# Gate stage of a residual block in one fixed order on four engines, with 23 instead of 19 chunks of the first expert product ahead

## The chip, the core and the metric

The kernel runs on one core of a Trainium2 chip. The metric is the device time of one execution in microseconds (us); three runs of the kernel before gave 1525.38, 1526.84 and 1527.6, their median is 1526.84.

## What is computed

Input is one sequence of 512 tokens of width 1024, in fp32. The block adds to it a mixture of spatial gating and banded attention, and then a PEER layer, which is where the change lies:

```python
def block(xb):                                   # for each of four blocks of 128 tokens
    q = (xb @ w_query).reshape(128, 8, 2, 128)
    sc = einsum('thpd,hpkd->thpk', q, sub_keys)
    s_top, i_top = top_k(sc, 16)
    cand = s_top[:, :, 0, :, None] + s_top[:, :, 1, None, :]        # 256 sums per head
    best, pos = top_k(cand, 16)
    eidx = ...                                   # i_top of one half * 128 + i_top of the other, at pos
    g = softmax(best)
    h = gelu(einsum('thkd,td->thk', expert_u[eidx], xb))
    return einsum('thk,thkd->td', g * h, expert_v[eidx])
```

There are 8 heads, 128 keys in each half of a head and so 16384 experts; a token uses 16 of them per head.

## The kernel before

**The work.** Tokens lie in four tiles of 128. For tiles 1 to 3 (384 tokens) the PEER layer is dense: the hidden value of all 16384 experts is computed, multiplied by a gate that is zero for experts not chosen, and multiplied by all rows of `expert_v`. For tile 0 the chosen rows are gathered from memory instead (`gather_u`, `gather_v`, lines 777 to 792, tile `row`, a ring of ROW buffers; POOL issues a gather, DVE reads the row). Of tile 3 the last 64 tokens get their hidden values by gathers too, early, in the gate stage (`gather_early` and `dots_early`, lines 472 and 481, tile `rowe`, a ring of four buffers): 64 gathers in all. The first product therefore covers 320 tokens.

**The products.** Every fp32 product is three products of a rounded part hi and a rest lo. `load_split` (lines 110 to 118) brings a weight tile of 512 KB by SP's DMA queue into `raw`, ACT writes hi (line 116) and DVE or POOL writes lo (line 117, "the split"). There are three raw and five hi and lo buffers. The first product has 64 chunks of two tiles of 128 experts. A tile is 24 matmuls of 128x320 (lines 132 to 134) and a gelu on ACT (line 518), which leaves it in an `act` buffer. The second product (lines 811 to 847) takes a chunk of act, multiplies it by the gates `gc` (line 825), makes hi and lo of it (`wh` line 826, `wl` lines 827 and 832), and adds 36 matmuls of 128x512 into six accumulators (`pa`, `px`).

**The stages.** First the mixture (not touched). Then the routing: for each head `candidates` makes the scores and the best 16 keys of both halves and, in between, one chunk of the first product; `choose` finds the best 16 of the sums, one head later. Behind the last choice (head 7) comes the gate stage: 48 steps of 8 tokens. A step makes two one-hots from the chosen experts' numbers, `bm` for the lower 7 bits (DVE line 689, then multiplied by the gate on POOL, line 690) and `am` for the upper (DVE line 697; on odd steps below SOON = 28 it is ACT, lines 694 and 695), multiplies them on PE (line 704), copies the result to `gst` (ACT, line 707), and every fourth step 2 MB of gst go to memory (`gd`, line 710, ACT's queue). With the steps go early gathers and their reads, and tiles of the first product: nine chunks come with the routing and its start, and ten more, up to AHEAD = 19, here. `gates_of` (line 661) turns a token tile's experts and gates by transposes (line 671) ahead of its 16 steps. Last comes the stage of the second products: each chunk's second product, then the first product of the chunk AHEAD later, and beside them the routing of tile 0 (`route_gathered`, in two parts) and its 256 gathers. A second product needs `gc`, which SP's queue reads back from gd (768 KB for two chunks, line 814).

**What sets the order.** PE runs in the order in which the program is written, in the gate stage and behind it. On DVE, ACT, POOL and SP a scheduler places instructions by its own estimate of when they are ready; each engine and each DMA queue then runs its own list in that order. In the gate stage, PE's list has BRIDGE = 4 tiles of the first product ahead of the first transposes, then ten over steps 0 to 27; the last six (LAST = 3 chunks) are written behind the steps and the scheduler puts them among the later ones:

```python
want = (len(early) + max(0, SOON - n) - 1) // max(1, SOON - n)    # early gathers of step n
gather_early(want)
...
while filled < min(last, begun + (last - begun) * (n + 1) // SOON):   # tiles up to step n
    next(fill)
    filled += 1
```

Of the kernel before, what the change touches and what calls it, by code (L numbers as in the profile page):

```python
# [26 lines left out]
NH = 8  # L27
# [30 lines left out]
ROW = 6  # L58
ROWE = 4
LAGE = 2  # L60
BRIDGE = 4
EARLY = 3
LEAD = 2
SOON = 28
AHEAD = 19
LAST = 3
FILL = 1
# [3 lines left out]
ROUTE = 8  # L71
GB = 4
TC = 8
TG = 32
# [8 lines left out]
def hybrid_block(tc, x, ln1, w_in, gng, wsT, bsb, qkg, bias, w_out, ln2, wq, skT, uT, ud, vd, out):  # L83
    nc = tc.nc
    ctx = ExitStack()
    with ctx:
# [408 lines left out]
        def weights_early():  # L495

            own = slice(P - UX, P)
            d = du.rearrange("p (a k) -> p a k", k=TOPK)
            nc.vector.tensor_copy(dots[own, :, 0, :], d[own])
            nc.scalar.dma_start(dots[own, :, 1, :], d[0:P - UX])  # L500
            nc.scalar.activation(dots[own], dots[own], AF.Gelu_apprx_tanh)
            nc.vector.tensor_tensor(gate[own, TT - 1, :], gate[own, TT - 1, :],
                                    dots[own].rearrange("p a b k -> p (a b k)"), op=ALU.mult)

        def first_product(c):
            for _ in first_products(c, nc.vector):
                pass

        def first_products(c, eng, whole=False):
            act = actp.tile([P, BC, NDU], F32, name="act", tag="act", bufs=AHEAD + 1)  # L510
            acts[c] = act
            for b in range(BC):
                hi, lo = load_split(uT[c * BC + b], eng, b=P)
                ps = pu()
                for k in range(KT):
                    x2 = (xbh[:, k, T0:T0 + NDU], xbl[:, k, T0:T0 + NDU]) if whole else (xch[:, k, :], xcl[:, k, :])
                    mm3(ps[:, :NDU], (hi[:, k, :], lo[:, k, :]), x2, k == 0, k == KT - 1)
                nc.scalar.activation(act[:, b, :], ps[:, :NDU], AF.Gelu_apprx_tanh)  # L518
                yield
# [25 lines left out]
        def pairs(pool, top, pos, n):  # L545
# [12 lines left out]
            tree = pool.tile([P, n, TOPK, 32], F32, name="tree", tag="tree", bufs=1)  # L558
            nc.gpsimd.tensor_copy(tree, cand[:, 1, :, None, 0:32].to_broadcast([P, n, TOPK, 32]))
            return cand, tree  # L560

        def choose(pool, cand, tree, n, best, to, mask):

# [32 lines left out]
        def candidates(h):  # L596
# [14 lines left out]
            fill = itertools.chain(*[first_products(len(acts) + i, nc.gpsimd, True) for i in range(FILL)])  # L611
# [18 lines left out]
        for _ in first_products(0, nc.vector, True):  # L630
            pass
        cands = []
        for h in range(NH + 1):
# [4 lines left out]
            if h < NH:  # L638
                cands.append(candidates(h))
            if h > 0:  # L640
# [107 lines left out]
        for _ in fill:  # L748
            pass
# [167 lines left out]
```

## Time and profile before

| | |
|---|---|
| median of three runs | 1526.84 us |
| the profiled execution: its own time | 1521.59 us |
| the profiled execution: its span, first to last instruction | 1519.8 us |
| PE busy | 1401.5 us (92%) |
| DVE busy | 1174.2 us (77%) |
| ACT busy | 628.8 us (41%) |
| POOL busy | 659.5 us (43%) |
| moved by DMA | 396.77 MB, mean 261 GB/s |
| mean granted clock of PE | 0.972 of 2.4 GHz |

The profile is that of one execution. Its span is what all times in the rows are measured in; 1.8 us of the execution's own time lie outside it. The shares are averages over stages with different limits, so rows of single stretches tell more than these do: the routing ends near 454 us, the gate stage near 645, and from 661 to the end only second and first products and the gathers of tile 0 run.

### The profile page before, as it was taken

What the parts mean: (1) busy time and instruction counts of PE and PEld (TensorE: products, weight loads), DVE (VectorE), ACT (ScalarE), POOL (GpSimd) and SP (SyncE); (2) the same over time, 40 slices, a digit from 0 to 9 for tenths busy, and PEclk for the clock granted to TensorE, in tenths of its full rate; (3) what the DMA queues carried; (4) which work ended last, traced back from release to release, by engine and by line L of the source; (5) the groups of instructions that cost most, each with busy time, mean ns of one, the idle gap of its engine ahead of it and who ended that gap; (6) DMA issues with size and microseconds to landing.
All of it is one profiled execution on the core that took longest, in us unless ns stands there. A gap on an engine that the chain in (4) does not pass through costs nothing.

```text
span 1519.8 us, 21632 instructions
## 1 busy us (share of the span) xinstructions
PE 1401.5 (92%) x7801; PEld 1236.7 (81%) x7801; DVE 1174.2 (77%) x2342; ACT 628.8 (41%) x1052; POOL 659.5 (43%) x434
## 2 busy tenths in 40 slices
PE   7999999989738679869999999999999999999988
PEld 6886678978728679859888898989898989888876
DVE  5437454879999888759998888888887888867774
ACT  5457544332237665424343334333333333333331
POOL 0000025566538755504645654665445554524420
PEclk9999999999978899979999999999999999999999
DMA  5352234467558968767989999899999999977972
GB/s 181 110 180 70 94 132 150 125 200 236 172 192 273 339 211 249 208 207 266 375 284 367 347 366 375 328 357 367 349 337 352 341 350 331 349 261 295 343 271 103
DMA packets 163419, 396.77 MB, mean 261 GB/s; under 512 B 12080, under 2 KB 74544, under 8 KB 163312
## 3 DMA queue, kind: packets, MB, share of 16 engines
q1 hardware_dynamic: 65968, 200.30, 37.5%
q0 software_dynamic: 46432, 168.60, 29.9%
q10 hardware_dynamic: 50912, 26.49, 6.2%
q8 instruction: 61, 1.00, 0.2%
q14 instruction: 46, 0.38, 0.1%
HBM read 363.86 MB, written 31.46 MB: 260 GB/s over the span
## 4 chain that ended last, share of the span: by engine, by line
PE 63%; DVE 17%; DMA 9%; issue 6%; ACT 3%; POOL 2%; DVEq 0%; SPq 0%; POOLq 0%
PE pu L132 8%; PE pu L134 8%; PE pu L133 8%; PE pa L842 6%; PE pa L843 6%; PE pa L846 6%; DMA rowe<-in_ud,eui 3%; DMA gc<-gd 3%; PE px L846 3%; PE px L842 3%; PE px L843 3%; PE pa L704 2%; PE pa L132 2%; PE pa L134 2%; PE pa L133 2%
## 5 line engine op out<-in xcount | busy, mean ns | idle before, releaser
L116 ACT ACTIVATE hi<-raw 128x1024 fp32r<-128x1024 f32 x300 | 317.8, 1060 | 596.0 <-DMA raw<-in_vd 179.4
L117 DVE TENSOR_TENSOR lo<-raw,hi 128x1024 fp32r<-128x1024 f32 x268 | 332.6, 1242 | 100.0 <-ACT hi L116 97.5
L790 POOL DMA_INDIRECT row<-in_vd,eint x128 | 212.9, 1663 | 195.8 <-DVE acc L792 167.8
L132 PE MATMUL pu<-xch,hi 128*128 128x320 f32 x880 | 273.6, 311 | 4.3 <-ACT act L518 4.2
L134 PE MATMUL pu<-xch,lo 128*128 128x320 f32 x880 | 271.9, 309 | 3.0 <-DVE lo L117 2.8
L133 PE MATMUL pu<-xcl,hi 128*128 128x320 f32 x880 | 271.8, 309 | 0.0
L779 POOL DMA_INDIRECT row<-in_ud,eint x128 | 181.3, 1417 | 180.4 <-DVE row L781 145.7
L842 PE MATMUL pa<-hi,wh 128*128 128x512 f32 x512 | 201.1, 393 | 0.0
L843 PE MATMUL pa<-lo,wh 128*128 128x512 f32 x512 | 200.6, 392 | 0.0
L132 PEld LDWEIGHTS pu<-xch,hi 128*128 128x128 f32 x880 | 166.0, 189 | 7.5 <-ACT act L518 5.6
L134 PEld LDWEIGHTS pu<-xch,lo 128*128 128x128 f32 x880 | 165.9, 189 | 4.0 <-DVE lo L117 4.0
L133 PEld LDWEIGHTS pu<-xcl,hi 128*128 128x128 f32 x880 | 166.1, 189 | 1.6
L792 DVE SCALAR_TENSOR_TENSOR acc<-row,hw,acc 128x1024 f32<-128x1024 f32 x128 | 164.2, 1283 | 0.2
L846 PE MATMUL pa<-hi,wl 128*128 128x512 f32 x512 | 158.8, 391 | 0.4 <-DVE wl L832 0.4
L781 DVE SCALAR_TENSOR_TENSOR row<-row,xb 128x1024 f32<-128x1024 f32 x128 | 155.7, 1219 | 2.4 <-DMA row<-in_ud,eint 2.4
L704 PE MATMUL pa<-bm,am 128*128 128x128 f32 x768 | 101.0, 292 | 36.3 <-DVE bm L689 12.2
L704 PEld LDWEIGHTS pa<-bm,am 128*128 128x128 f32 x768 | 96.4, 205 | 40.5 <-issue 14.1
L825 DVE TENSOR_TENSOR act<-act,gc 128x320 f32<-128x320 f32 x128 | 54.8, 486 | 88.2 <-DMA gc<-gd 88.2
L842 PE MATMUL px<-hi,wh 128*128 128x512 f32 x256 | 100.9, 394 | 15.9 <-ACT wh L826 15.9
L846 PEld LDWEIGHTS pa<-hi,wl 128*128 128x128 f32 x512 | 96.5, 189 | 21.6 <-DVE wl L832 1.1
L842 PEld LDWEIGHTS pa<-hi,wh 128*128 128x128 f32 x512 | 96.9, 189 | 20.6
L843 PEld LDWEIGHTS pa<-lo,wh 128*128 128x128 f32 x512 | 96.9, 189 | 20.6
(211 smaller groups left out, 2521.6 us busy)
## 6 DMA issues: line engine op xcount, KB each, us to landing
raw<-in_uT SPq DMA_DIRECT2D x128, 512.0 KB
raw<-in_vd SPq DMA_DIRECT2D x128, 512.0 KB
gd<-gst ACTq DMA_DIRECT2D x12, 2048.0 KB
gc<-gd SPq DMA_DIRECT2D x32, 768.0 KB
raw<-in_w_in SPq DMA_DIRECT2D x20, 512.0 KB
raw<-in_wq SPq DMA_DIRECT2D x16, 512.0 KB
raw<-in_w_out SPq DMA_DIRECT2D x8, 512.0 KB
bt<-in_bias SPq DMA_DIRECT2D x8, 256.0 KB
```

The costliest lines, as they stand in the source:

```text
L116: nc.scalar.activation(hi, raw, AF.Copy)
L117: eng.tensor_tensor(lo, raw, hi.bitcast(F32), op=ALU.subtract)
L132: nc.tensor.matmul(ps, lh[0], rh[0], start=first, stop=False)
L133: nc.tensor.matmul(ps, lh[0], rh[1], start=False, stop=False)
L134: nc.tensor.matmul(ps, lh[1], rh[0], start=False, stop=last)
L704: nc.tensor.matmul(ps[:, i * P:(i + 1) * P], am[:, 4 * q + i, :], bm[:, 4 * q + i, :], start=True, stop=True)
L779: nc.gpsimd.indirect_dma_start(out=row, out_offset=None, in_=ud, in_offset=bass.IndirectOffsetOnAxis(ap=eint[:, j:j + 1], axis=0))
L790: nc.gpsimd.indirect_dma_start(out=row, out_offset=None, in_=vd, in_offset=bass.IndirectOffsetOnAxis(ap=eint[:, j:j + 1], axis=0))
L792: nc.vector.scalar_tensor_tensor(acc0, row, hw[:, j:j + 1], acc0, op0=ALU.mult, op1=ALU.add)
L842: nc.tensor.matmul(accs[t][half], wh[:, b, tok], w[b][0][:, ds_], start=first, stop=False)
L843: nc.tensor.matmul(accs[t][half], wh[:, b, tok], w[b][1][:, ds_], start=False, stop=False)
L846: nc.tensor.matmul(accs[t][half], wl[:, b, tok], w[b][0][:, ds_], start=False, stop=last)
```

## The change

- AHEAD is 23 instead of 19, with act buffers to match; those of slot 14 and up lie in a pool that is opened behind the routing. SOON is 25. ROW, the ring of tile 0's gathers, is 4 instead of 6.
- Eight tiles of the first product (BRIDGE = 8) are written ahead of the last choice instead of four behind it, with their splits on POOL. All splits of the gate stage are on POOL; before they were DVE's.
- In the gate stage not PE alone but PE, DVE, ACT and POOL keep the order of the program. For that the functions are cut: `indices_of` and `gates_of`, `second_one_hot` (bm, ahead of a step's products) and `first_one_hot` (am, behind them), `weights_early` in two parts (its copy between partitions on POOL's queue), `split_tile`, `multiply_tile` and `activate_tile`.
- Of the 20 tiles left for the gate stage, 14 go at a pace of SLOW = 20 in SOON = 25 steps, so that they end in step 17; the last six stand behind the last products.
- Gates go out every second step as 1 MB (TG 16 instead of 32) and come back as 1.5 MB for four chunks (GB 8 instead of 4).
- The routing of tile 0 runs in four parts, behind chunks 0, 4, 8 and 12, instead of two behind 0 and 8. The copy that starts the tree of a choice is made at the choice and not with the candidates.

```diff
-ROW = 6
+ROW = 4
-BRIDGE = 4
+BRIDGE = 8
+SLOW = 20
-SOON = 28
-AHEAD = 19
+SOON = 25
+AHEAD = 23
-ROUTE = 8
-GB = 4
+PARTS = 4
+ROUTE = 4
+GB = 8
-TG = 32
+TG = 16
...
             if h < NH:
                 cands.append(candidates(h))
+            else:
+                for _ in first_products(len(acts) * BC, BRIDGE, nc.gpsimd, True):
+                    pass
             if h > 0:
...
-        for _ in range(BRIDGE):
-            next(fill)
-        filled += BRIDGE
-        begun = filled
-        with tc.manual_schedule(engines={mybir.EngineType.PE}):
+        def split_next():
+            nonlocal split
+            if split < AHEAD * BC:
+                split_tile(split, nc.gpsimd)
+                split += 1
+        engines = {getattr(mybir.EngineType, e) for e in ("PE", "DVE", "Activation", "Pool")}
+        with tc.manual_schedule(engines=engines):
+            ff[0] = indices_of(GT)
+            split_next()
+            gs[0] = gates_of(GT, ff.pop(0))
+            split_next()
             for n in range(steps + LEAD):
...
+                if n < steps:
+                    bms[n] = second_one_hot(gs[t], c)
                 if n >= LEAD:
...
-                    products(*hots.pop(m), m % per, st)
+                    products(ams.pop(m), bms.pop(m), m % per, st)
                     if (m + 1) * TC % TG == 0:
                         store(m * TC // TG, st)
-                while filled < min(last, begun + (last - begun) * (n + 1) // SOON):
-                    next(fill)
-                    filled += 1
-        for _ in fill:
-            pass
+                while begun:
+                    activate_tile()
+                if n < steps:
+                    ams[n] = first_one_hot(gs[t], c, n % 2 == 1 and n < SOON)
+                dots_early(LAGE)
+                if n < steps:
+                    gather_early((len(early) + max(0, SOON - n) - 1) // max(1, SOON - n))
...
+                here = SLOW * (n + 1) // SOON if n < SOON else \
+                    SLOW + (AHEAD * BC - i0 - SLOW - LAST * BC) * (n + 1 - SOON) // (steps - SOON)
+                while split - len(ready) - i0 < min(here, AHEAD * BC - i0 - LAST * BC):
+                    multiply_tile()
+                    split_next()
+            while ready:
+                multiply_tile()
+                split_next()
...
-            n = NH // 2
+            n = NH // PARTS
...
-                if c % ROUTE == 0 and c < 2 * ROUTE:
+                if c % ROUTE == 0 and c < PARTS * ROUTE:
                     route_gathered(c // ROUTE)
```

What stands where is seen from the engines' lists. A row is line, operation, out<-in, shape and a count where it repeats. Lines of the changed program lie some lines further down: 472 is 475, 481 is 484, 117 is 120, 689 is 714, 690 is 716, 697 is 730.

POOL's list at the start of the gate stage, before: the last gathers of the routing, then the first one-hots' multiplications.

```order
L472 DMA rowe<-in_ud,eui 128x1024 x3
L487 DMA eu<-eidx 64x16
L472 DMA rowe<-in_ud,eui 128x1024 x5
L690 TENSOR_TENSOR bm<-bm,gt 128x1024 x3
L472 DMA rowe<-in_ud,eui 128x1024
L690 TENSOR_TENSOR bm<-bm,gt 128x1024
L472 DMA rowe<-in_ud,eui 128x1024 x3
```

The same place after the change:

```order
L716 TENSOR_TENSOR bm<-bm,gt 128x1024
L475 DMA rowe<-in_ud,eui 128x1024 x4
L716 TENSOR_TENSOR bm<-bm,gt 128x1024
L475 DMA rowe<-in_ud,eui 128x1024 x2
L120 TENSOR_TENSOR lo<-raw,hi 128x1024
L716 TENSOR_TENSOR bm<-bm,gt 128x1024
L475 DMA rowe<-in_ud,eui 128x1024 x2
L120 TENSOR_TENSOR lo<-raw,hi 128x1024
```

The first multiplication stood behind eight gathers of the last index set; now it stands ahead of nearly all of them, and gathers and splits alternate with the multiplications.

DVE's list at the end of the last choice, before; L481 reads an early row, L117 is a split, L689 is the first one-hot.

```order
L481 SCALAR_TENSOR_TENSOR rowe,du<-rowe,px 128x1024
L583 COPY eidx<-tree 128x3x16
L481 SCALAR_TENSOR_TENSOR rowe,du<-rowe,px 128x1024
L666 CAST ei<-eidx 128x128
L481 SCALAR_TENSOR_TENSOR rowe,du<-rowe,px 128x1024
L667 TENSOR_SCALAR ii<-ei 128x128
L668 TENSOR_SCALAR ii<-ei 128x128
L117 TENSOR_TENSOR lo<-raw,hi 128x1024
L492 CAST eui<-eu 128x16
L669 CAST ff<-ii 128x256
L481 SCALAR_TENSOR_TENSOR rowe,du<-rowe,px 128x1024 x2
L689 TENSOR_TENSOR bm<-iota_k,pa 128x1024
```

After the change:

```order
L599 COPY_PREDICATED tree<-pa,tree 128x48x2
L599 COPY_PREDICATED tree<-pa,tree 128x48
L601 COPY eidx<-tree 128x3x16
L495 CAST eui<-eu 128x16
L689 CAST ei<-eidx 128x128
L690 TENSOR_SCALAR ii<-ei 128x128
L691 TENSOR_SCALAR ii<-ei 128x128
L692 CAST ff<-ii 128x256
L714 TENSOR_TENSOR bm<-iota_k,pa 128x1024
```

Reads and the split have left this place: the steps of the choice and of the numbers' conversion now follow each other up to the first one-hot.

SP's queue at the end of the gate stage, before, with the buffers' numbers; `in_uT` are tiles of the first product, `in_vd` of the second.

```order
L115 DMA raw_5757<-in_uT 128x1024
L115 DMA raw_5807<-in_vd 128x1024
L115 DMA raw_5813<-in_vd 128x1024
L115 DMA raw_5864<-in_uT 128x1024
L115 DMA raw_5896<-in_uT 128x1024
L115 DMA raw_6034<-in_vd 128x1024
L115 DMA raw_6040<-in_vd 128x1024
L115 DMA raw_6091<-in_uT 128x1024
L115 DMA raw_6123<-in_uT 128x1024
L814 DMA gc_5805<-gd_3987 128x1536
L814 DMA gc_6155<-gd_3987 128x1536
```

After the change:

```order
L118 DMA raw_5225<-in_uT 128x1024
L118 DMA raw_5903<-in_uT 128x1024
L118 DMA raw_5934<-in_uT 128x1024
L118 DMA raw_5967<-in_uT 128x1024
L873 DMA gc_6076<-gd_4247 128x3072
L873 DMA gc_6647<-gd_4247 128x3072
L118 DMA raw_5999<-in_uT 128x1024
L118 DMA raw_6078<-in_vd 128x1024
L118 DMA raw_6084<-in_vd 128x1024
```

The loads of the first vd tiles stood well ahead of the read-back of the gates; now they stand behind it and behind one more uT tile, and the read-back is twice as large.

## Rows read from the trace of the kernel before

**Rows 1.** The page: the engines' shares of the chain of work that ended last, and the conversion to hi among its costliest groups (line, engine, operation, out<-in, count | busy us, mean ns of one | idle us before them and what ended it).

```profile
PE 63%; DVE 17%; DMA 9%; issue 6%; ACT 3%; POOL 2%; DVEq 0%; SPq 0%; POOLq 0%
...
L116 ACT ACTIVATE hi<-raw 128x1024 fp32r<-128x1024 f32 x300 | 317.8, 1060 | 596.0 <-DMA raw<-in_vd 179.4
```

**Rows 2.** The table of stretches: from and to in us, length, then for each engine its busy us and in brackets its instructions, the mean granted clock of PE as a share of 2.4 GHz, the mean busy share of the 16 DMA engines, GB/s.

```profile
395.00:455.00 60.00, 27.22 (x159) 25.60 (x157) 58.76 (x230) 17.81 (x32) 21.04 (x20) 0.80 0.54 182
455.00:545.00 90.00, 67.48 (x483) 66.07 (x483) 80.81 (x105) 57.31 (x132) 69.67 (x48) 0.87 0.92 309
545.00:645.00 100.00, 89.19 (x675) 86.59 (x675) 78.74 (x69) 60.19 (x119) 53.08 (x28) 0.97 0.72 211
645.00:661.00 16.00, 0.13 (x1) 0.13 (x1) 1.85 (x6) 1.82 (x4) 0.00 (x0) 0.63 0.80 257
661.00:1519.80 858.80, 848.12 (x4464) 751.20 (x4464) 704.94 (x1099) 315.23 (x443) 398.07 (x258) 0.99 0.86 319
```

**Rows 3.** The view of waits of PE between 380 and 720 us: engine, output and line <- what it waited for: us in total, times, longest us.

```profile
PE pa L671 <- issue: 18.6, 1, 18.6
PE px L842 <- ACT wh L826: 15.9, 1, 15.9
PE pa L704 <- DVE bm L689: 12.2, 1, 12.2
```

**Rows 4.** The timeline of PE: start, duration, engine, line, operation. The first two rows are the first and the last of the 24 matmuls of a tile of the first product, the third is the first one behind the last of the choices' products; the last two are the first matmuls of two neighbouring groups of six of a second product.

```profile
394.12 0.30 PE L132 MATMUL pu<-xbh,hi 128*128 128x320 f32 x1
...
397.48 0.31 PE L134 MATMUL pu<-xbh,lo 128*128 128x320 f32 x1
...
404.58 0.61 PE L132 MATMUL pu<-xbh,hi 128*128 128x320 f32 x1
...
667.59 0.39 PE L842 MATMUL px<-hi,wh 128*128 128x512 f32 x1
...
668.95 0.39 PE L842 MATMUL pa<-hi,wh 128*128 128x512 f32 x1
```

**Rows 5.** DVE in the last choice of experts: groups by line, operation and shape between 396.4 and 453.5 us (columns as in rows 1), and from its timeline the first one-hot behind them.

```profile
L481 DVE SCALAR_TENSOR_TENSOR rowe<-rowe,px 128x1024 f32<-128x1024 f32 x12 | 14.6, 1220 | 1.0 <-DMA rowe<-in_ud,eui 1.0
L117 DVE TENSOR_TENSOR lo<-raw,hi 128x1024 fp32r<-128x1024 f32 x7 | 8.5, 1210 | 0.0
...
453.54 1.22 DVE L689 TENSOR_TENSOR bm<-iota_k,pa 128x1024 f32<-128x1024 f32 x1
```

**Rows 6.** The timeline of DVE in the later gate steps; bm and am alternate between the two rows, each of the eight instructions behind the one before.

```profile
603.41 1.22 DVE L689 TENSOR_TENSOR bm<-iota_k,pa 128x1024 f32<-128x1024 f32 x1 [0.53 <-PE pa L704]
...
611.34 1.22 DVE L697 TENSOR_TENSOR am<-iota_k,pa 128x1024 f32<-128x1024 f32 x1
```

**Rows 7.** The timeline of POOL: the first, the 25th and the 48th multiplication of a one-hot by its gate.

```profile
454.85 1.92 POOL L690 TENSOR_TENSOR bm<-bm,gt 128x1024 f32<-128x1024 f32 x1
...
560.28 1.90 POOL L690 TENSOR_TENSOR bm<-bm,gt 128x1024 f32<-128x1024 f32 x1 [0.76 <-DVE bm L689]
...
639.14 1.90 POOL L690 TENSOR_TENSOR bm<-bm,gt 128x1024 f32<-128x1024 f32 x1 [0.36 <-DVE bm L689]
```

**Rows 8.** The timeline: a split on POOL; a split on DVE and the issue of a gather on POOL beside it, and the next gather; a gather of the last stage whose issue waited for nothing but POOL itself.

```profile
393.60 2.42 POOL L117 TENSOR_TENSOR lo<-raw,hi 128x1024 fp32r<-128x1024 f32 x1
...
414.80 1.22 DVE L117 TENSOR_TENSOR lo<-raw,hi 128x1024 fp32r<-128x1024 f32 x1
...
415.15 1.70 POOL L472 DMA_INDIRECT rowe<-in_ud,eui  x1 [0.79 <-DVE rowe L481]
...
417.43 0.95 POOL L472 DMA_INDIRECT rowe<-in_ud,eui  x1 [0.58 <-DVE rowe L481]
...
808.53 0.94 POOL L779 DMA_INDIRECT row<-in_ud,eint  x1 [0.30 <-issue]
```

**Rows 9.** The chain of work that ended last, in order of time (start, us, what): a gather of an early row; then the end of the gate stage, from its last products to the second product.

```profile
500.10 7.80 DMA rowe<-in_ud,eui
...
640.25 4.75 PE pa L704 x40
...
645.63 8.66 DMA gd<-gst
...
654.50 4.33 DMA gc<-gd
...
660.87 0.79 PE px L842
```

**Rows 10.** POOL between 455 and 545 us, by line and shape (columns as in rows 1; behind the second bar the idle time before them and what ended it).

```profile
L690 POOL TENSOR_TENSOR bm<-bm,gt 128x1024 f32<-128x1024 f32 x20 | 38.7, 1950 | 2.7 <-DVE bm L689 2.5
L472 POOL DMA_INDIRECT rowe<-in_ud,eui x28 | 31.1, 1112 | 14.4 <-DVE rowe L481 10.4 <-issue 2.9 <-DVE ff L669 0.5
```

**Rows 11.** The timeline of DVE: the read of the row whose gather is the last of rows 8; and two rows of POOL's waits over the whole span (columns as in rows 3).

```profile
817.64 1.21 DVE L781 SCALAR_TENSOR_TENSOR row<-row,xb 128x1024 f32<-128x1024 f32 x1
...
POOL row L790 <- DVE acc L792: 167.8, 88, 11.1
POOL row L779 <- DVE row L781: 145.7, 67, 10.3
```

**Rows 12.** The timeline of DVE: the instruction that makes the masks of a choice, in the choice before the last and in the last.

```profile
393.39 2.97 DVE L569 TENSOR_TENSOR pa<-bpos,bits 128x288 uint32<-128x288 uint32 x1
...
436.55 0.46 DVE L569 TENSOR_TENSOR pa<-bpos,bits 128x288 uint32<-128x288 uint32 x1
```

More of the change, by code (lines that the diff above doesn't have):

```diff
@@ L493, in ready_early, with weights_early @@
             early.extend(range(js.start, js.stop))
-        def weights_early():
+        def weights_early(part):
             own = slice(P - UX, P)
             d = du.rearrange("p (a k) -> p a k", k=TOPK)
[L499 to L503, printed above, removed]
@@ L505, in first_product @@
-        def first_product(c):
-            for _ in first_products(c, nc.vector):
-                pass
[L509 to L518, printed above, removed]
+            if part == 0:
+                nc.vector.tensor_copy(dots[own, :, 0, :], d[own])
+                nc.gpsimd.dma_start(dots[own, :, 1, :], d[0:P - UX])
+            else:
+                nc.scalar.activation(dots[own], dots[own], AF.Gelu_apprx_tanh)
+                nc.vector.tensor_tensor(gate[own, TT - 1, :], gate[own, TT - 1, :],
+                                        dots[own].rearrange("p a b k -> p (a b k)"), op=ALU.mult)
@@ new lines, in hybrid_block, with split_tile, multiply_tile @@
+        ready, begun, more = [], [], []
+        def split_tile(i, eng):
+            c, b = divmod(i, BC)
+            if b == 0:
+                slot = c % (AHEAD + 1)
+                acts[c] = (actp if slot < SOME else more[0]).tile([P, BC, NDU], F32, name="act", tag=f"act{slot}")
+            ready.append((c, b, load_split(uT[i], eng, b=P)))
+        def multiply_tile(whole=False):
+            c, b, (hi, lo) = ready.pop(0)
+            ps = pu()
+            for k in range(KT):
+                x2 = (xbh[:, k, T0:T0 + NDU], xbl[:, k, T0:T0 + NDU]) if whole else (xch[:, k, :], xcl[:, k, :])
+                mm3(ps[:, :NDU], (hi[:, k, :], lo[:, k, :]), x2, k == 0, k == KT - 1)
+            begun.append((c, b, ps))
@@ L610, in candidates @@
                 qts.append(qt)
-            fill = itertools.chain(*[first_products(len(acts) + i, nc.gpsimd, True) for i in range(FILL)])
+            fill = first_products((len(acts)) * BC, FILL * BC, nc.gpsimd, True)
             next(fill, None)
@@ L627, in candidates @@
             return pairs(rq, top, pos, ND)
-        for _ in first_products(0, nc.vector, True):
+        for _ in first_products(0, BC, nc.vector, True):
             pass
@@ L642, in hybrid_block @@
                 mask = pa()[:, 0:6 * ND * TOPK].bitcast(U32)
-                choose(rq, *cands.pop(0), ND, gate[:, GT:, hs], eidx[:, GT:, hs], mask)
+                tree = rq.tile([P, ND, TOPK, 32], F32, name="tree", tag="tree", bufs=1)
+                choose(rq, cands.pop(0), ND, gate[:, GT:, hs], eidx[:, GT:, hs], mask, tree)
                 if h % 2 == 0:
@@ L669, in gates_of @@
             nc.vector.tensor_copy(ff, ii)
+            return ff
+        def gates_of(t, ff):
             ps = pa()
```

81 lines of the change are left out of this document (51 added, 30 removed).

## The prediction

> **What bounds the kernel now.** I read the page first: PE carries 63% of the chain that ended last, DVE 17% [rows 1]. That is an average over stages, so the next view is the table of stretches [rows 2]. From 661 us to the end PE is busy 848 of 859 us at a granted clock of 0.99: there only less PE work helps. In the 266 us before that it is busy only 184, at clocks of 0.63 to 0.97. So work of PE that is moved from behind 661 to ahead of it is worth its full time, as long as the front does not grow by it. The view of PE's waits names the holes [rows 3]: 18.6 us ahead of the first transposes of the gate stage (PE's program order makes it wait for the last choice of experts, which DVE makes), 15.9 us ahead of the second product (for wh, and behind it the read-back of the gates), and inside the gate steps waits for the one-hots, 12.2 us at once on bm.
>
> What a tile of the first product costs: 24 matmuls whose starts run from 394.12 to 397.48, so 0.146 us apart and 3.52 us a tile [rows 4]. One pair of a second product takes 6 matmuls in 1.36 us [rows 4], 8.2 us a chunk.
>
> **The change, term by term.** The sum is made in the profiled execution (span 1519.8, own time 1521.59); the median of the runs shown, 1526.84, lies 5.25 above that, and I carry the difference over to it.
>
> *Behind 661.* 38 tiles stand ahead of the first second-product matmul before (19 chunks of two). After the change it is 46, of which the order on PE leaves 4.17 of the last six ahead of that matmul and the rest behind: 44.17. So 6.17 tiles x 3.52 = **-21.7 us**.
>
> *The last choice.* Between 396.4 and 453.5 DVE is never idle for more than a us and does, besides the choice, 7 splits and 12 reads of early rows [rows 5]; both leave it. Such instructions start 1.13 us apart where DVE waits for nothing (603.41 to 611.34, seven steps) [rows 6], so that is 19 x 1.13 = 21.6 us, so DVE would reach the first bm at 432 instead of 453.54. But PE now runs nine tiles there in place of five: from 404.58 on [rows 4] 9 x 3.52 gives 436.3, and the transposes stand behind them in its order. With transposes, two copies and bm the first multiplication of POOL comes at 439.5 instead of 454.85 [rows 7]: **-15.4 us**. Eight splits on POOL at 2.42 [rows 8] hide below the tiles (19 of 32 us).
>
> *Steps 0 to 24.* This is the term that decides. In the order POOL now does, per step, one multiplication, two gathers and in 14 of 25 steps a split; 48 of the 64 early gathers stand behind the first multiplication (28 before, the others went out under the last choice). Prices: multiplication 1.90 [rows 7]; gather 0.95 and 0.30 to the next issue, split 2.42 [rows 8]. 25 x 1.90 + 48 x 1.25 + 14 x 2.42 = 47.5 + 60 + 33.9 = 141 us. DVE's part, 38 one-hots and 52 reads at 1.14, is 103 us; PE's, 25 times 16 products at 0.119 [rows 9] and 14 tiles at 3.52, is 97: POOL becomes the bound. The gathers also form a ring of four buffers: read 1.2 [rows 5], notice 0.6 [rows 8], then 7.8 from issue to landing [rows 9], so 10 us per two steps at least; only in the seven steps without splits is that more than POOL's own time, about 7 us more in all. 148 us, against the 107.3 that multiplications 1 to 25 take now (454.85 to 562.18, the end of the 25th) [rows 7]: **+40.7 us**.
>
> The 0.95 is a choice. The gather at 415.15, beside the split that DVE began at 414.80 (two SBUF operands), takes 1.70; the one at 417.43, after that split, takes 0.95 [rows 8]. The splits leave DVE in this stage, so I take 0.95; at 1.70 the term would grow by 48 x 0.75 = 36 us. The Trainium skill agrees in part (SBUF — State Buffer, Who interferes with whom): a DVE instruction with two SBUF inputs contends with GpSimd's reads, one with a single SBUF input does not.
>
> *Steps 25 to 47.* The tiles of PE and the splits of DVE that stand here now go. What stays on DVE is bm and am, at the same 1.13 apart [rows 6], 2.27 a step. The store is halved to 1 MB but two buffers still turn, now each two steps: 2 MB lands in 8.66 us [rows 9], so 1 MB in 4.3 (half) to 5.3 (if 2 us of it are fixed); bounds 2.27 to 2.67 a step, I take 2.4. 23 x 2.4 = 55.2 against 78.9 (562.18 to 641.04) [rows 7]: **-23.7 us**.
>
> *From the last multiplication to the second product.* Before: 641.04 to 660.87, 19.8 us [rows 7, 9]. After: 4.6 us of products and copy, as now (645.63), 5.3 for the store, then SP sends two gc of 1.5 MB, one more uT and only then the first vd tile, whose raw was ahead of gc before. 0.75 MB landed 4.33 us after its issue [rows 9]. 4.2 MB at 0.336 MB a us (309 GB/s at a DMA share of 0.92 [rows 2]) need 12.5 us; I add 2 to land and 1.06 for hi [rows 1]: 25.5 us, **+5.7**. Were vd not the last, it would be about as now; were the transfers at the 0.26 MB a us of the hole now [rows 2], 29. The 4.17 tiles fill 14.7 us of it, so the long hole of PE shrinks to about 7 us; their worth is counted in the first term.
>
> Sum: -21.7 - 15.4 + 40.7 - 23.7 + 5.7 = **-14.4 us**: span 1505.4, and 1512.4 for the median.
>
> At nothing I cost: the route in four parts (DVE is busy 705 of 859 us behind 661 [rows 2]; the same searches, some 25 small instructions more), gc in sixteen loads, the place of the last choice's tree, and POOL's earlier order, where PE loses little now. Their cover is DVE's 150 us of slack in that stage; if it goes, splits come late and PE waits.
>
> **The rivals.**
> 1. *POOL meets its waits as now.* From 455 to 545 it is busy 69.7 of 90 us [rows 2] with 20 multiplications and 28 gathers; in 10.4 us it waits for rows to be read [rows 10]. With 2.9 of issue that is an efficiency of 81%. Steps 0 to 24 would take 141 / 0.81 = 174, +26: about 1539. For it: in-order POOL now has one more thing to wait for (hi from ACT). Against it: DVE, 81 of 90 busy now, is at 70% afterwards.
> 2. *Four row buffers bind behind 661 (slower).* The gathers of the last token tile get 4 buffers in place of 6. The shortest time from issue to a read that did not wait is 9.1 us (808.53 to 817.64) [rows 8, 11]; with read 1.2 and notice 0.6 four gathers turn in at most 10.9 us, 2.7 each, and 5.4 gathers per 15.2 us chunk need one in 2.8. From a turn of 12.2 us on the 256 gathers set the end: they start near 708, and at 12.8 (3.2 each) last 819 us, plus 12 to the output: span 1539, 1546 for the median. For it: DMA is 0.86 busy in that stage, and gathers queue with raw and gc. Against it: POOL waits 314 us for rows to be read [rows 11], so rows lie ready long before they are used.
> 3. *POOL overlaps better.* With the 0.30 between gathers hidden and no ring the 25 steps take 127 us: 1491.
> 4. *Splits on POOL slow the last choice.* The DVE instruction that makes the masks took 2.97 us beside a split on POOL and 0.46 alone [rows 8, 12]. Six places of the last two choices read two SBUF tiles; 2.5 us at each is 15, less the 4 to 5 by which DVE is ahead of PE's nine tiles: +10, 1522. The Trainium skill's same section states this as an exclusive lock in which the later one waits; it speaks against putting ten splits beside the choice, and the trace's 2.97 agrees.
>
> That the splits would not move to POOL is no rival: the order has them there.
>
> **How the numbers follow.** Forecast 0.45 at **1512.4** (own range 1503 to 1521 from the bounds of the small terms), rival 1 0.17, rival 2 0.18, rival 3 0.10, rival 4 0.10. The range goes from half of rival 3 to nearly all of rival 2: **1494 to 1545**, which leaves out about 2 in 10. A measurement can tell 0.2%, 3 us, from no change. Faster: the forecast, rival 3 and half of rival 4, 0.59. Same: the rest of 4 and the near ends of 1 and 2, 0.11. Slower: 0.30.
>
> **What would show it.** First multiplication of POOL at 436 to 445; POOL 90% busy or more up to the 25th, which ends near 588; gathers of 0.95 in the gate stage; then a step each 2.4 us; the second product's first matmul near 668 with a hole of 5 to 9 us ahead of it on PE; behind it PE over 98% busy. Wrong it is if the 25th multiplication comes after 605 (rival 1), if DVE waits for rows behind 700 and PE for splits (rival 2), or if POOL starts after 450 (rival 4).

## The result and the profile after

The changed kernel takes 1517.28 us (median of eight runs, 1514.74 to 1521.09) against 1524.57 for the kernel before: a ratio of 0.9948, with a 95% interval from 0.9932 to 0.9965. The forecast was 14.4 us faster and the measured gain is 7.3 in the medians, 5.6 in the spans of the two profiled executions (1519.8 and 1514.2).

The table of stretches of the changed kernel, cut at the ends of its stages (columns as in [rows 2]; the last row is a piece of the one above it):

```profile
400.00:445.00 45.00, 36.01 (x230) 35.25 (x229) 30.44 (x111) 15.33 (x28) 18.93 (x10) 0.92 0.29 93
445.00:584.00 139.00, 104.48 (x693) 100.70 (x694) 104.01 (x139) 83.93 (x178) 125.61 (x87) 0.89 0.95 311
584.00:642.00 58.00, 49.27 (x378) 45.24 (x377) 56.90 (x58) 27.87 (x50) 45.37 (x26) 0.97 0.80 229
642.00:669.30 27.30, 19.03 (x123) 18.04 (x121) 11.83 (x22) 11.06 (x17) 9.58 (x4) 0.89 0.78 279
669.30:1514.20 844.90, 828.43 (x4312) 730.27 (x4312) 699.46 (x1123) 312.06 (x436) 388.63 (x260) 0.99 0.87 321
760.00:900.00 140.00, 131.96 (x694) 116.25 (x693) 128.48 (x261) 52.85 (x74) 72.20 (x47) 0.98 0.87 318
```

POOL's timeline after the change: the split ahead of the first multiplication, and the first, 25th and 48th multiplication, which answer to [rows 7].

```profile
442.84 2.41 POOL L120 TENSOR_TENSOR lo<-raw,hi 128x1024 fp32r<-128x1024 f32 x1 [14.11 <-ACT hi L119]
445.20 1.90 POOL L716 TENSOR_TENSOR bm<-bm,gt 128x1024 f32<-128x1024 f32 x1
...
582.13 1.92 POOL L716 TENSOR_TENSOR bm<-bm,gt 128x1024 f32<-128x1024 f32 x1
...
640.03 1.90 POOL L716 TENSOR_TENSOR bm<-bm,gt 128x1024 f32<-128x1024 f32 x1 [0.37 <-DVE bm L714]
```

PE's timeline there: the two starts behind a wait between the last multiplication and the second product.

```profile
663.61 0.64 PE L135 MATMUL pu<-xch,hi 128*128 128x320 f32 x1 [5.44 <-ACT act L530]
...
669.33 0.80 PE L902 MATMUL px<-lo,wh 128*128 128x512 f32 x1 [2.86 <-DVE lo L120]
```

From these starts the five terms of the sum can be read off, each beside its forecast:

| term | forecast | in the two traces |
|---|---|---|
| first multiplication (454.85 before) | 439.5, -15.4 | 445.20, -9.7 |
| multiplications 1 to 25 (107.3) | 148, +40.7 | 445.20 to 584.05: 138.9, +31.5 |
| multiplications 26 to 48 (78.9) | 55.2, -23.7 | 584.05 to 641.93: 57.9, -21.0 |
| to the second product (19.8) | 25.5, +5.7 | 641.93 to 669.33: 27.4, +7.6 |
| from there to the end (858.9) | -21.7 | 669.33 to 1514.2: 844.9, -14.1 |

Taken together the four terms of the front came out as forecast: the second product starts to run on at 669.33, where the sum has 668.2. What is missing is missing behind it. The page's shares of the chain that ended last are taken over the whole span, so they cannot name the stage, but they show that less of the chain is PE's work: PE had 63% of it [rows 1], and now has this:

```profile
PE 47%; DVE 20%; DMA 14%; issue 10%; POOL 7%; ACT 2%; SPq 0%; DVEq 0%; POOLq 0%; ACTq 0%
```

### The profile page after: what moved, and what is told of

Read it like the earlier page. It is cut to its first block, busy times and chain, and to the rows that moved or that the text cites. A ratio compares the mean times of both kernels' runs of the same rounds, so it can differ in the third digit from the quotient of the medians.

```text
span 1514.2 us, 21710 instructions
## 1 busy us (share of the span) xinstructions
PE 1414.0 (93%) x7801; PEld 1243.9 (82%) x7801; DVE 1161.0 (77%) x2360; ACT 631.6 (42%) x1040; POOL 709.4 (47%) x465
## 4 chain that ended last, share of the span: by engine, by line
PE 47%; DVE 20%; DMA 14%; issue 10%; POOL 7%; ACT 2%; SPq 0%; DVEq 0%; POOLq 0%; ACTq 0%
PE pu L135 6%; PE pu L137 6%; PE pu L136 6%; DMA row<-in_vd,eint 5%; PE pa L901 4%; PE pa L902 4%; PE pa L905 4%; DMA row<-in_ud,eint 3%; DMA rowe<-in_ud,eui 3%; PE pa L135 2%; PE pa L137 2%; PE pa L136 2%; DMA gc<-gd 2%; PE px L902 2%; PE px L905 2%
## 5 line engine op out<-in xcount | busy, mean ns | idle before, releaser
L120 DVE TENSOR_TENSOR lo<-raw,hi 128x1024 fp32r<-128x1024 f32 x240 | 292.5, 1220 | 85.0 <-ACT hi L119 84.0
L849 POOL DMA_INDIRECT row<-in_vd,eint x128 | 194.6, 1521 | 183.4 <-DVE acc L851 156.7
L137 PE MATMUL pu<-xch,lo 128*128 128x320 f32 x816 | 253.2, 310 | 12.1 <-POOL lo L120 7.7
L135 PE MATMUL pu<-xch,hi 128*128 128x320 f32 x816 | 254.9, 312 | 6.8 <-ACT act L530 6.8
L136 PE MATMUL pu<-xcl,hi 128*128 128x320 f32 x816 | 252.4, 309 | 0.0
L120 POOL TENSOR_TENSOR lo<-raw,hi 128x1024 fp32r<-128x1024 f32 x60 | 144.3, 2413 | 98.1 <-ACT hi L119 97.6
L137 PEld LDWEIGHTS pu<-xch,lo 128*128 128x128 f32 x816 | 154.3, 189 | 15.4 <-POOL lo L120 9.3
L135 PEld LDWEIGHTS pu<-xch,hi 128*128 128x128 f32 x816 | 154.6, 189 | 9.9 <-ACT act L530 8.3
L136 PEld LDWEIGHTS pu<-xcl,hi 128*128 128x128 f32 x816 | 154.3, 189 | 1.6
L902 PE MATMUL px<-lo,wh 128*128 128x512 f32 x256 | 101.6, 397 | 6.5 <-DVE lo L120 6.5
```

The costliest lines, as they stand in the source:

```text
L120: eng.tensor_tensor(lo, raw, hi.bitcast(F32), op=ALU.subtract)
L135: nc.tensor.matmul(ps, lh[0], rh[0], start=first, stop=False)
L136: nc.tensor.matmul(ps, lh[0], rh[1], start=False, stop=False)
L137: nc.tensor.matmul(ps, lh[1], rh[0], start=False, stop=last)
L849: nc.gpsimd.indirect_dma_start(out=row, out_offset=None, in_=vd, in_offset=bass.IndirectOffsetOnAxis(ap=eint[:, j:j + 1], axis=0))
L902: nc.tensor.matmul(accs[t][half], wh[:, b, tok], w[b][1][:, ds_], start=False, stop=False)
```

## The experiments

Ratios are against the kernel before, run beside each kernel on the same chip, with 95% intervals. Two questions were open: whether POOL really bounds steps 0 to 24, and what took 7 us behind 669.

### What sets the pace of steps 0 to 24

**Half of the splits on DVE**, and **all of them on DVE**:

```diff
-                split_tile(split, nc.gpsimd)
+                split_tile(split, nc.vector if split % 2 else nc.gpsimd)   # half
+                split_tile(split, nc.vector)                               # all
```

> Of the 20 splits of the gate stage every second one is DVE's again, so 7 of the 14 of steps 0 to 24. Theory A (POOL is the bound of these steps): multiplications 1 to 25 take 139 - 7 x 2.4 = 122 us, the second product starts 12 to 17 us earlier, ratio about 0.985. Rival B (the ring of four early-row buffers and the landing of gathers set the pace): 139 us stay within 4, ratio 0.993 to 0.996. Rival C (a split on DVE lengthens the gather issued beside it from 0.95 to 1.7 us): 7 x 0.75 = 5 us of the gain are lost, 127 us, ratio 0.988.

> All 20 splits of the gate stage are DVE's, as in the kernel before. Theory A (POOL the bound with them): a step costs POOL 1.9 + 2 x 1.2, the ring of early rows 5.0, so multiplications 1 to 25 take about 120 to 125 us, DVE busy 121 of them: little or nothing more than with half of the splits, ratio 0.984 to 0.988. Rival B (ring): 139 us within 4. Rival C (contention of a two-operand split with gathers): 14 x 0.75 = 10 us back, about 132 us, ratio 0.991.

Half: 0.9940 [0.9920, 0.9959]; multiplications 1 to 25 took 140.0 us. All: 0.9911 [0.9892, 0.9929]; 139.8 us. The stretch of multiplications 1 to 25 with all splits on DVE (table of stretches):

```profile
445.31:585.15 139.84, 104.69 (x698) 101.82 (x699) 118.70 (x154) 84.15 (x177) 99.09 (x72) 0.89 0.92 310
```

POOL in the same stretch, by line and shape:

```profile
L475 POOL DMA_INDIRECT rowe<-in_ud,eui x47 | 51.4, 1095 | 40.3 <-DVE rowe L484 31.1 <-issue 6.8 <-DVE ei L689 1.1
L716 POOL TENSOR_TENSOR bm<-bm,gt 128x1024 f32<-128x1024 f32 x25 | 47.6, 1906 | 18.9 <-DVE bm L714 18.4
```

POOL is busy 99 us instead of 125 and the stretch is as long as before: A, taken alone, falls. The time that the splits gave back has become 31.1 us of waiting for rows to be read, that is, for one of the four early-row buffers (the 18.4 us of the second row lie ahead of the first multiplication, outside the stretch). Both lengths are B's and not C's; that the second ratio is still the 0.991 that C had comes from the last stage (see "Not settled" below). So B is there, but is it B instead of A, or B beside A?

**Six early-row buffers**, with the splits on DVE, and with the splits left on POOL:

```diff
-ROWE = 4
+ROWE = 6
```

> The kernel with all splits of the gate stage on DVE (multiplications 1 to 25 took 139.8 us, as with POOL's splits, with POOL busy 99 and DVE 119 of them), and ROWE 6 instead of 4: six buffers for early rows. Theory D (the 16 DMA engines set the pace: 43.4 MB in these 140 us, their busy share 0.92): 139.8 stays within 4, a gather's landing grows from 6.7 us to 9 or more. Rival B (the ring of four rows, issue to landing to read to issue, sets it): the stage shortens to what DVE needs, about 122 us, and the ratio to about 0.982.

> The changed kernel with ROWE 6 instead of 4 and nothing else (splits stay on POOL). Ring theory B with POOL next behind it: POOL is busy 125.5 us of the 25 steps, so they take 127 to 132 us instead of 138.9, ratio 0.987 to 0.990. Theory A alone (POOL was the bound already): 137 to 139, ratio 0.994 to 0.996. DMA theory D: 139, too.

With the splits on DVE: 0.9834 [0.9814, 0.9853]. With them on POOL: 0.9941 [0.9918, 0.9965]. The stretch of multiplications 1 to 25, first of the kernel with both edits:

```profile
450.54:571.38 120.84, 98.84 (x699) 95.87 (x699) 118.12 (x152) 83.62 (x178) 97.26 (x70) 0.94 0.99 354
```

Then of the kernel with six buffers alone:

```profile
448.85:583.15 134.30, 103.92 (x691) 100.25 (x692) 103.38 (x139) 83.09 (x176) 123.60 (x85) 0.91 0.94 315
```

And POOL's waits in that stretch:

```profile
POOL rowe L475 <- issue: 8.5, 38, 0.3
POOL rowe L475 <- DVE rowe L484: 1.4, 5, 0.3
```

Neither edit alone gives much (139.8 and 134.3 us against 138.9); both together give 120.8, and then DVE is busy 118 of them. So two limits of nearly the same height lie on top of each other: POOL's own list (123.6 busy and 8.5 of gaps between gathers are 132.1 of 134.3 us) and the ring. The 127 to 132 us that B had for six buffers alone did not come. D falls with the first of these rows: nearly the same gathers (45 issued in the stretch instead of 47), with more of them under way, move 354 GB/s instead of 310.

Two things keep these lengths from being read too closely. With six buffers the first multiplication also came later, by 3.7 us with the splits on POOL and by 5.2 with them on DVE, so the 25th ends 0.9 and 13.8 us earlier. And the kernel put together further down, which has the same two edits in these steps, took 125.3 us in its one trace.

**Four tiles in place of eight beside the last choice** adds four splits to POOL's list in these steps and takes four tiles from PE's ahead of them:

```diff
-BRIDGE = 8
+BRIDGE = 4
```

> The changed kernel with BRIDGE 4 instead of 8: four tiles less beside the last choice, 18 instead of 14 in the gate steps, four more splits on POOL there. PE's five tiles end at 425.5, DVE's choice at 428.8, so the first multiplication comes at 434 instead of 445. Theory B (ring: the steps' pace does not hang on four more splits): 25 steps take 139 to 142 us, the second product starts 8 to 11 us earlier, ratio 0.988. Theory A (POOL): 139 + 4 x 2.4 = 148 us, ratio 0.994. Rival (DVE's choice ends later without tiles to hide it, first multiplication at 443 or later): ratio above 0.996.

0.9896 [0.9877, 0.9915]. The first multiplication came at 429.93, and the stretch of 25 from there is this:

```profile
429.93:579.73 149.80, 117.87 (x805) 113.44 (x803) 109.14 (x144) 89.03 (x185) 134.96 (x91) 0.92 0.93 307
```

It is 10.9 us longer for four more splits (4 x 2.4 = 9.6), as A has it: POOL's list sets the end while the splits are on it. The start came 15.3 us earlier, one more than the four tiles' 14.1, so the eight tiles beside the choice did delay it. The ratio is below A's 0.994 in part because the start had been expected at 434.

**Gathers sent earlier**, in the routing:

```diff
-EARLY = 3
+EARLY = 6        # and 8 in the second run
```

> The changed kernel with EARLY 6 instead of 3: 28 of the 64 early gathers stand ahead of the first multiplication instead of 16, 36 behind it instead of 48. Theory D (DMA bound, 0.31 MB a us): 12 gathers of 0.52 MB less are 20 us, multiplications 1 to 25 take about 119 us; the 12 reads cost DVE 14 us in the routing, of which it has 11 idle, so the gate stage starts 3 us later; ratio about 0.984. Rival B (ring): two gathers a step less often, 25 steps take 120 to 130 us. Rival A2 (the wait chain through one-hots and products, 5.6 us a step whatever the gathers): 135 to 139 us, ratio 0.995.

> As the run with EARLY 6, with EARLY 8: 36 gathers ahead of the first multiplication, 28 behind it, as many as in the kernel before. Theory D: 20 gathers less are 34 us, so 105 us for multiplications 1 to 25 (107 before); 20 reads cost DVE 23 us in the routing, 11 of it idle time, first multiplication at about 457; ratio about 0.981. Rival A2: 130 us or more and ratio above 0.995.

0.9967 [0.9954, 0.9979] and 1.0001 [0.9985, 1.0017]: the ratios are A2's (0.995 or above), the lengths are not. D's 119 and 105 us did not come either; only B's 120 to 130 us, given for EARLY 6, did. With EARLY 6 the first multiplication came at 458.4 and the 25 took 125.9 us, with EARLY 8 at 468.4 and 125.4. The stretch with EARLY 8:

```profile
468.41:593.77 125.36, 94.96 (x683) 92.81 (x683) 84.23 (x105) 80.01 (x173) 107.25 (x68) 0.90 0.85 268
```

The reads cost the last choice more than its idle time (13 us later for 12 of them, 23 for 20), and with 28 gathers in the stretch in place of 48 it is no shorter than with 36. POOL is busy 107 of 125 there and the DMA engines 0.85; what else holds these steps at 125 us stays open.

### What is missing behind the second product

DVE's waits for gathered rows from 669 us on, in the changed kernel:

```profile
DVE acc L851 <- DMA row<-in_vd,eint: 43.3, 30, 4.2
DVE row L840 <- DMA row<-in_ud,eint: 34.1, 31, 5.3
```

That is 77 us. In the kernel before, DVE's waits from 661 us on hold one such line:

```profile
DVE row L781 <- DMA row<-in_ud,eint: 2.4, 4, 1.4
```

DVE runs its list in order, so splits and wl stand behind such a read; PE is idle 8.0 us between 760 and 900, against 1.2 before. PE's waits in that stretch say what for, all 8.0 us of it:

```profile
PE pu L137 <- DVE lo L120: 4.4, 4, 2.0
PE px L902 <- DVE lo L120: 3.6, 3, 2.3
```

One of them in order of time: DVE's read of a late row, the split behind it, and PE's matmul that waited for this split.

```profile
802.43 1.23 DVE L840 SCALAR_TENSOR_TENSOR row<-row,xb 128x1024 f32<-128x1024 f32 x1 [1.37 <-DMA row<-in_ud,eint]
...
803.59 1.22 DVE L120 TENSOR_TENSOR lo<-raw,hi 128x1024 fp32r<-128x1024 f32 x1
...
804.86 0.50 PE L902 MATMUL px<-lo,wh 128*128 128x512 f32 x1 [0.92 <-DVE lo L120]
```

Theory R puts it down to the ring of four row buffers, theory P to the routing in four parts, which keeps DVE busy 128 of these 140 us. Six buffers don't fit beside 24 act buffers, so R was tried on the kernel before. One thing that run does not have: in the changed kernel the tree of each routing part lies in the same ring (tag `row` in `route_gathered`), which leaves three buffers for gathers meanwhile. No run separates this from the ring's size.

**The kernel before with four row buffers:**

```diff
-ROW = 6
+ROW = 4
```

> The kernel before with ROW 4 instead of 6 and nothing else. Theory R (four buffers for the rows of tile 0 make DVE wait for rows, splits come late, PE waits): DVE's waits for rows behind 661 us grow from 3 to 60 us or more, PE's idle time between 760 and 900 from 1.2 to 5 to 8 us, ratio 1.003 to 1.005. Rival P (the routing in four parts, not the buffers): PE's idle time stays under 2 us, ratio 0.999 to 1.001.

1.0083 [1.0067, 1.0098], 12.6 us slower, about twice what R expected. DVE's waits for rows behind 661 in that kernel:

```profile
DVE acc L792 <- DMA row<-in_vd,eint: 28.0, 21, 3.1
DVE row L781 <- DMA row<-in_ud,eint: 18.5, 22, 1.8
```

Its stretch from 760 to 900, and below it the same one of the kernel before:

```profile
760.00:900.00 140.00, 135.54 (x738) 120.56 (x737) 120.57 (x207) 51.45 (x72) 70.50 (x45) 1.00 0.90 330
```

```profile
760.00:900.00 140.00, 138.81 (x758) 124.03 (x757) 125.80 (x204) 55.79 (x78) 76.82 (x49) 1.00 0.91 338
```

PE's idle time there goes from 1.2 to 4.5 us, and DVE's waits for rows from 2.4 to 46.5, both a little less than R expected. Over the whole last stage PE's idle time goes from 10.7 to 27.5 us, in the longest of the six executions (1543.59, where their median is 1538.05). The kernels differ in the ring alone, so R is shown: four buffers are enough to make DVE wait and PE stand.

**The four parts twice as far apart:**

```diff
-ROUTE = 4
+ROUTE = 8
```

> ROUTE is 8 instead of 4: the four parts of the routing of tile 0 stand behind chunks 0, 8, 16 and 24 instead of 0, 4, 8 and 12; ROW stays 4. Rival P of the run with six row buffers (DVE too full between 760 and 900): the same work is spread over twice the time, DVE's share between 760 and 900 falls from 0.92 to about 0.88, PE's idle time there from 8 to 3 us or less, the ratio to 0.991 to 0.993. Theory R (buffers): no change within 2 us, ratio 0.994 to 0.996.

0.9900 [0.9883, 0.9918], some 7 us below the changed kernel's ratio, where P had it. Its profiled execution was the longest of its four (1516.97 against 1509.81 to 1511.17), and its stretch from 760 to 900 speaks against P:

```profile
760.00:900.00 140.00, 131.77 (x706) 116.93 (x705) 123.99 (x231) 52.71 (x73) 74.03 (x47) 0.99 0.86 314
```

DVE's busy time fell as P has it (124.0 us instead of 128.5), but PE is idle 8.2 us there as before. So P is not shown; the shorter times of the other three executions fit it, and what shortened them stays open.

**Put together:** splits on DVE, six early-row buffers, the routing in eight parts behind chunks 0 to 28, and the memory that this saves spent on a fifth row buffer:

```diff
-ROWE = 4
+ROWE = 6
-ROW = 4
+ROW = 5
-PARTS = 4
+PARTS = 8
-                split_tile(split, nc.gpsimd)
+                split_tile(split, nc.vector)
-                   tree.rearrange("p (h k m) -> p h k m", h=n, k=TOPK))
+                   tree[:, 0:n * TOPK * 32].rearrange("p (h k m) -> p h k m", h=n, k=TOPK))
```

> Put together: splits of the gate stage on DVE, ROWE 6, the routing of tile 0 in eight parts behind chunks 0, 4, ... 28 (PARTS 8), and with the memory that saves ROW 5. Theory R: five buffers and a thinner routing shorten DVE's waits for rows (56 us with ROW 4 in the run that had the first two edits) to 20 or less, PE's idle time behind the second product falls from 17 to 10 us, ratio 0.978 to 0.980. Rival (the waits are the gathers' share of a full DMA, whatever the ring): ratio 0.982 to 0.984.

0.9741 [0.9722, 0.9760], 14 us below the run that had the first two of these edits. DVE's waits for rows in that run, ahead of the last edits:

```profile
DVE acc L851 <- DMA row<-in_vd,eint: 33.5, 26, 4.0
...
DVE row L840 <- DMA row<-in_ud,eint: 22.8, 26, 2.8
```

And with them:

```profile
DVE row L840 <- DMA row<-in_ud,eint: 5.0, 7, 1.4
...
DVE acc L851 <- DMA row<-in_vd,eint: 4.9, 5, 1.4
```

The stretches of the kernel put together: multiplications 26 to 48, everything behind the first matmul of the second product, and 760 to 900.

```profile
574.50:633.40 58.90, 48.60 (x371) 44.37 (x371) 57.88 (x60) 27.28 (x49) 45.34 (x26) 0.97 0.76 218
656.24:1489.40 833.16, 824.83 (x4317) 729.36 (x4316) 709.37 (x1216) 321.63 (x447) 391.51 (x264) 0.99 0.87 326
760.00:900.00 140.00, 137.70 (x754) 123.31 (x753) 127.20 (x240) 56.22 (x79) 72.45 (x49) 1.00 0.92 348
```

DVE's waits for rows go from 56 to 10 us, PE is idle 8.3 us in the last stage instead of 17.3 (843.7 less 826.4 in the run with two edits), and 2.3 instead of 7.7 between 760 and 900. The gain is more than expected and comes by the expected way: the rival's 0.982 to 0.984 fell. How much of it is the fifth buffer's and how much the thinner routing's is not separated.

### The way into the second product

**Two tiles behind the last products instead of six**, on the kernel put together:

```diff
-LAST = 3
-SLOW = 20
+LAST = 1
+SLOW = 14
-                split_tile(split, nc.vector)
+                split_tile(split, nc.vector if split < i0 + SLOW + 2 else nc.gpsimd)
```

> As the run put together, with LAST 1 and SLOW 14: two tiles instead of six behind the last products, four more in steps 25 to 47 (their splits on POOL), and so the first two vd tiles are loaded ahead of the read-back of the gates. Forecast: from the last multiplication to a second product that runs on, 18 to 20 us instead of 27; steps 25 to 47 grow by 0 to 4 us; ratio 0.003 to 0.005 below that run. Rival: the four splits and tiles in the later steps cost what the end gains, ratio equal within 0.001.

0.9797 [0.9775, 0.9819], slower than the kernel put together, and by more than the rival had it. Multiplications 26 to 48:

```profile
569.00:634.20 65.20, 56.63 (x441) 54.25 (x440) 59.32 (x61) 30.50 (x57) 52.21 (x29) 0.97 0.77 223
```

PE's wait ahead of its second product:

```profile
PE px L901 <- ACT wh L885: 10.0, 1, 10.0
```

The first two vd tiles had been sent by 624 us, and PE still stood 10.0 us, for wh: store, read-back and the product with the gates set this place, not vd. The four tiles that filled the hole now cost 6.3 us among the steps, where the same stretch has 58.9. In the two traces the steps ahead of these are 4.7 us shorter and the stage behind them 3.6 longer, so the 6.3 alone don't make up the loss.

**BRIDGE 4 on the kernel put together**, since that edit gave 8 us while POOL was the bound:

> The run put together (ratio 0.974) with BRIDGE 4 instead of 8. The first multiplication comes 15 us earlier, as in the run of the changed kernel with BRIDGE 4 (430 instead of 445). The steps get four tiles more, with splits on DVE: DVE is busy 118 of 125 us there, so 4 x 1.14 = 5 us more, and 2.1 MB more at 0.34 MB a us, 6 us: multiplications 1 to 25 take 130 to 132 us. Forecast: ratio 0.967 to 0.970. Rival: the DMA engines, 0.98 busy there, take 10 us or more for it and for the gathers that start closer together, ratio 0.972 or above.

0.9669 [0.9650, 0.9687], median 1475.07: the fastest here, 2.8% below the changed kernel. The stretch of multiplications 1 to 25, from 434.41:

```profile
434.41:557.67 123.26, 108.57 (x798) 106.02 (x796) 122.35 (x156) 89.14 (x186) 98.49 (x70) 0.98 1.00 363
```

It carries four tiles more and is no longer for it: 123.3 us against 125.3, where 130 to 132 had been expected; DVE is busy 122 of them, the DMA engines 1.00 at 363 GB/s.

## Why the prediction was right, and where it was not

**Steps 0 to 24**, the term that decided, is right in its cause and 9 us too long. POOL's groups in that stretch of the changed kernel:

```profile
L716 POOL TENSOR_TENSOR bm<-bm,gt 128x1024 f32<-128x1024 f32 x25 | 47.6, 1904 | 0.2
L475 POOL DMA_INDIRECT rowe<-in_ud,eui x47 | 45.4, 965 | 12.9 <-issue 8.2 <-DVE rowe L484 3.8 <-DVE bm L714 0.5
L120 POOL TENSOR_TENSOR lo<-raw,hi 128x1024 fp32r<-128x1024 f32 x15 | 35.7, 2377 | 14.4 <-ACT hi L119 14.1
```

47.6 us of multiplications and 35.7 of 15 splits (the first began ahead of the stretch) are the prices of the sum; the gather at 0.965 is the 0.95 that was chosen, so the choice against 1.70 was right, and so was its reason: with the splits back on DVE the mean gather took 1.095. That agrees with the rule cited from the Trainium skill (SBUF — State Buffer, Who interferes with whom), by which a DVE instruction with two SBUF inputs contends with GpSimd's reads; that it lengthens the issue of a gather is this case's measurement. What was too dear is the gap: 0.30 was put behind each of 48 gathers, but it lies between two that follow each other, 8.2 us in all in place of 14.4. The ring was counted as 7 us on top; by the sum's own prices it is 4.2 (seven steps, 5.0 for the ring against 1.90 and 2 x 1.25), and POOL's waits for reads are 3.8. That a faster POOL would have run into the ring at the same height was not seen: rival 3 took the ring away with the gaps and priced 127 us, but with six buffers the gaps did not hide, and the steps took 134.3.

**The last choice** came 5.7 us later than forecast. PE's timeline and ACT's name the larger part:

```profile
423.25 0.63 PE L135 MATMUL pu<-xbh,hi 128*128 128x320 f32 x1 [7.57 <-ACT act L530]
```

```profile
419.98 0.52 ACT L608 ACTIVATE ex<-ex 128x384 f32<-128x384 f32 x1 [8.72 <-DVE ex L607]
420.41 1.04 ACT L119 ACTIVATE hi<-raw 128x1024 fp32r<-128x1024 f32 x1
```

ACT's list has the exponentials of the softmax, which wait 8.7 us for DVE, ahead of a conversion to hi and of a gelu, and PE stands 7.6 us for that gelu in the middle of its nine tiles. The sum let the tiles run on; they ended at 439.6 (445.20 less the 5.6 us of transposes, copies, bm and split) instead of 436.3. The rest is POOL's split ahead of the first multiplication (442.84, in the timeline above), 2.4 us that the sum left out.

Why DVE was late there is rival 4's mechanism, at another instruction than rival 4 priced. First POOL's splits and DVE's cast beside them, in order of time, then DVE's four casts of this line over the whole span (shortest, median and longest in ns):

```profile
395.74 7.10 POOL L120 TENSOR_TENSOR lo<-raw,hi 128x1024 fp32r<-128x1024 f32 x3
...
395.81 7.06 DVE L495 CAST eui<-eu 128x16 int32<-128x16 f32 x1
```

```profile
L495 DVE CAST eui<-eu x4: 154/1950/7062, 303.9 to 427.4; 128x16 int32<-128x16 f32 x4
```

A cast of 16 numbers a partition, 0.15 us at its shortest, took 7.06 us beside three splits on POOL and ended 0.03 us behind them. A copy (line 491) and the next cast also end 0.03 and 0.04 us behind a split of POOL. The first stands ahead of the whole last choice, so about 6.9 of the 8.7 us that ACT waited are its price (an estimate, 7.06 less 0.15), and PE's 7.6 us hang on them. The sign that was set for rival 4, a start after 450, did not come, because PE's tiles covered the rest; with four tiles beside the choice nothing covers it, and PE then waits 11 us ahead of the transposes. The longest cast takes 7.07 to 7.11 us in nine of the later kernels too; with EARLY 6 and 8 it takes 2.03 and 0.17 at most, but there the added reads hide what that is worth, and no run moved the cast alone.

The prediction has it from the Trainium skill that an instruction with a single SBUF input does not contend. That section makes this conditional: outside modes that copies and casts can enter. The cast has a single input, and its measured time decides here.

**Steps 25 to 47** were forecast at 2.4 us a step and took 2.5, with DVE busy 56.9 of 58 us: the bound is DVE's, as chosen, and not the store's.

**To the second product** 27.4 us instead of 25.5: right in size, and that is luck, for the reason was wrong. The sum had the load of vd as the last to arrive. Loading vd first did not shorten the hole; the path through store, read-back and wh alone took 23 us there (634.2 to 657.16), and it took 23 in the changed kernel, too (641.93 to 664.88, the first matmul of the second product). What follows in the changed kernel is again DVE's list: the split of the first vd tile stands behind seven products with the gates.

```profile
663.06 5.08 DVE L884 TENSOR_TENSOR act<-act,gc 128x320 f32<-128x320 f32 x7
668.07 3.55 DVE L120 TENSOR_TENSOR lo<-raw,hi 128x1024 fp32r<-128x1024 f32 x3
```

**Behind it** is the term that failed: -21.7 was forecast, -14.1 came. The moved tiles are there (PE is busy 828.4 us; 848.1 less 21.7 is 826.4), and PE's idle time grew from 10.7 to 16.5 us: 5.8 of the missing 7.6. The rest, some 2 us, is PE's own busy time; its granted clock from 760 to 900 is 0.98, where it was 1.00. The sum put nothing here for reads that come late, in a ring of four or beside a route in four parts ("At nothing I cost: the route in four parts"); its cover was DVE's 150 us of slack. DVE's list is in order, so slack on the average does not cover a read whose row is late. It is rival 2's mechanism, in the form that was to be looked for (DVE waiting for rows, PE for splits), with a small part of rival 2's price: what PE stood for was DVE's splits, not the end of the gathers (the last one goes out at 1465, 49 us ahead of the end). The point against rival 2, that POOL waits for reads and so rows lie ready, was drawn from six buffers and did not carry over to four.

The number came out 4.9 us below the measured median. Of the 8.8 us by which the profiled spans miss the sum's 1505.4, 7.6 lie behind the second product; the misses in the front (+5.7, -9.2, +2.7, +1.9) cancel to 1. Both this cancelling and the 3.9 us between 8.8 and 4.9 are luck: the sum carried over the 5.25 us by which the profiled execution of the kernel before lay under its median, and the changed kernel's lies only 1.4 under its own.

Not settled: the last stage is some 6 us shorter in the three kernels with half or all splits on DVE (843.6 to 843.7 us from the first matmul of the second product) than with all on POOL (847.6 to 852.7), though they have the same work there. Some 1.8 us of it is PE's wait for the first vd tile's split, 2.9 us with all splits on POOL and 1.0 to 1.1 in those three.

## What to carry to other kernels

Where an engine's list fills a stretch, ask for the next limit of the same height before spending effort on it: in these steps taking splits off POOL gave nothing, two more buffers 4.6 us at most, and both together 14 to 18. Size a ring of gathers by issue, landing under load, read and notice; where its reads stand in an in-order list with work that the critical engine needs, two buffers fewer cost 12.6 us here though the reader had slack on the average. Work that fills a hole is free only in that hole, and before work goes to POOL, look for copies and casts of DVE beside it: one of them cost about 6.9 us here.

## What was not expected of the hardware

The DMA engines were at a share of 0.92 to 0.95 in steps 0 to 24, and that looked like a limit; with six buffers in the ring they went to 0.99 and 354 GB/s, and in the last kernel to 1.00 and 363. A share below 1 by a few per cent left 14 to 17% of throughput to be had.

A DVE cast of 128x16 stood still for three splits of POOL in a row, 7.06 us instead of 0.15, with POOL's splits no longer for it (7.10 us for three).
